# x loaded by token halves, and two of three sums of squares taken in feature order

## The chip, the cores and the metric

One core of a Trainium2 chip runs the kernel. The metric is device time in microseconds (us) of one execution; three runs of the kernel before gave 864.88, 865.59 and 865.71.

## The reference, cut to what matters

The reference is a two-layer network on x (512 tokens of 1024 features) and ctx (256 tokens). The first layer is a retention mixer, the second a gMLP mixer. The change lies in the very first step of the first layer, the norm with its modulation, and in the projections that wait for it:

```python
def rmsnorm(x, g):
    xf = x.astype(F32)
    y = xf * lax.rsqrt(jnp.mean(xf * xf, axis=-1, keepdims=True) + NORM_EPS)
    return (y * g.astype(F32)).astype(x.dtype)
...
shift_x, scale_x, gate_x = jnp.split(silu_c @ ada_w[i] + ada_b[i], 3, axis=-1)
shift_c, scale_c, gate_c = jnp.split(silu_cc @ ada_w[i] + ada_b[i], 3, axis=-1)
hx = rmsnorm(x, norm_g[i]) * (1 + scale_x[:, None]) + shift_x[:, None]
hc = rmsnorm(ctx, norm_g[i]) * (1 + scale_c) + shift_c
```

Each token thus needs the sum of the squares of its 1024 features before anything of it can be projected.

## The kernel before, in words

x and ctx come with the features on the 128 partitions: eight feature tiles `kb` of 128, `KT` = 8. x's 512 tokens are two halves of 256 (`th` 0 and 1). Four tiles `xs` hold two feature tiles each, all 512 tokens; two tiles `cq` hold four feature tiles of ctx each.

**Exact products by splitting.** Weights and activations are split into a high part (a cast on ScalarE) and a low part (a subtraction on VectorE), and a product takes three matmuls (`mm3`, L126). `Stream` (L155) loads the weights as raw pieces and splits them ahead of their use; `w11` and `w12` are the first two pieces, cut by `cut` (L795) in slices since the first products want them early. Nearly every instruction is issued through `Queue`, so the profile puts it on L54.

**The first stage** (L812 to L913) works feature tile by feature tile. One turn for `kb` is:

- `ada0_mm` (L638): the modulation's columns of that tile, c and c_ctx against the ada weights, on TensorE; then a copy `adae` on ScalarE;
- `ada0_cols` (L654): transposes of `adae` on TensorE, sums over their groups and three small operations on VectorE, giving scale `gs0` and shift `sh0`;
- `come` (L751): for one or more halves, x times scale times `rs` (VectorE, `xs<-xs,gs,rs`), plus shift (ScalarE, `oA` or `oS` for the first and the second half), and the low part (VectorE);
- `plain` (L776): the products of that tile, for half `th` and piece `nh`, added up in four PSUM banks; `features_first` (L395) takes the three matmuls in another order than `features` (L385).

`rs[t]` is one over the root mean square of each token: t = 0 and 1 are x's halves, 2 is ctx. `half_rows` (L605) gets it by transposing four feature tiles at a time on TensorE (16 transposes for a half of x, 16 for ctx) and summing squares of 128 tokens' rows: on ScalarE (Square with an accumulator) for the one 128 tokens, on VectorE (`bn_stats`) for the other. `inverse` (L616) joins the sums, takes the root (ScalarE) and the reciprocal (VectorE). `spread` (L626) brings the 256 numbers to all partitions by two products with the identity matrix, and `copied` copies them out of PSUM.

**What sets the order.** In this stage the order on TensorE, ScalarE and VectorE is that of the text (`kept`): each engine is a queue, and what waits holds up all behind it. Loads are issued by SyncE in the text's order, eight in flight at most over SyncE and ScalarE. ada tiles 4, 5 and 6 use the memory of tiles 0, 1 and 2, so their loads wait for those tiles' products. Two small loads, `cv` (c and c_ctx) and `ident` (the identity matrix), go over ScalarE's queue. ScalarE loads a table, takes Silu of `cv`, and then loads the table that Square and Sqrt use. Ten products of ones warm TensorE up at the start (`fill`), six more stand ahead of the first real products.

In the text before, both halves' statistics come first; then each turn serves both halves: tile 0 of half 0, tile 0 of half 1, then their second weight piece, then tile 1 of both, and so on.

## Time and profile before

| | |
|---|---|
| median of three runs | 865.59 us (864.88 to 865.71) |
| the profiled execution's own time | 865.68 us |
| its span, first to last instruction | 863.8 us |
| mean granted TensorE clock | 0.998 |
| TensorE, VectorE, ScalarE busy | 854.3, 706.7, 479.5 us |
| loads of x: 4, 512 KB each | 5.5 us from issue to landing (median) |
| loads of ctx: 2, 512 KB each | 8.7 us |

A span begins with the first instruction; times in the timeline count from there. PE is TensorE's matmuls, PEld its weight loads, DVE is VectorE, ACT is ScalarE, SP is SyncE, POOL is GpSimd. In a timeline a row is start, duration, engine, line, operation, what it writes and reads, its shape and how many in a row; in brackets stands how long the engine was idle before and what ended that. A product in plain float32 shows as two records, one for each pass.

### The profile page before, as it was taken

What the parts mean: (1) busy time and instruction counts of PE and PEld (TensorE: products, weight loads), DVE (VectorE), ACT (ScalarE), POOL (GpSimd) and SP (SyncE); (2) the same over time, 40 slices, a digit from 0 to 9 for tenths busy, and PEclk for the clock granted to TensorE, in tenths of its full rate; (3) what the DMA queues carried; (4) which work ended last, traced back from release to release, by engine and by line L of the source; (5) the groups of instructions that cost most, each with busy time, mean ns of one, the idle gap of its engine ahead of it and who ended that gap; (6) DMA issues with size and microseconds to landing.
All of it is one profiled execution on the core that took longest, in us unless ns stands there. A gap on an engine that the chain in (4) does not pass through costs nothing.

```text
span 863.8 us, 17055 instructions
## 1 busy us (share of the span) xinstructions
PE 854.3 (99%) x6820; PEld 816.9 (95%) x6820; DVE 706.7 (82%) x996; ACT 479.5 (56%) x763; POOL 84.8 (10%) x127
## 2 busy tenths in 40 slices
PE   8999999999999999999999999999999999999997
PEld 7899999999999999899999899999999899899985
DVE  4799899869977985799787889998888478678895
ACT  5466644455355446567872559654667456255434
POOL 0001211211211011000001011111000000000110
PEclk9999999999999999999999999999999999999999
DMA  9945857866967796248486842657556156156522
GB/s 358 405 133 147 256 174 257 259 202 197 307 205 232 223 324 235 73 122 243 157 283 174 255 113 97 232 149 230 160 148 205 39 148 219 26 152 190 122 46 101
DMA packets 78990, 164.03 MB, mean 190 GB/s; under 512 B 8256, under 2 KB 35264, under 8 KB 78912
## 3 DMA queue, kind: packets, MB, share of 16 engines
q1 hardware_dynamic: 66144, 122.37, 42.2%
q0 software_dynamic: 12336, 40.38, 18.6%
q8 instruction: 53, 0.87, 0.4%
q10 hardware_dynamic: 432, 0.20, 0.1%
q14 instruction: 25, 0.20, 0.1%
HBM read 124.65 MB, written 24.12 MB: 172 GB/s over the span
## 4 chain that ended last, share of the span: by engine, by line
PE 95%; DMA 3%; ACT 1%; DVE 1%; issue 0%; DVEq 0%; SPq 0%; ACTq 0%
PE pst L54 95%; DMA ada_w<-in_ada_dram 2%; DMA cq<-in_cT_dram 1%; DMA cv<-in_cv_dram 0%; DVE o L54 0%; ACT junk L54 0%; DVE ada_h L54 0%; ACT og L54 0%; ACT ada_h L54 0%; ACT fss L54 0%; ACT o L54 0%; DVE fss L54 0%; DVEq L1946 0%; SPq L54 0%; ACT ones_r L54 0%
## 5 line engine op out<-in xcount | busy, mean ns | idle before, releaser
L54 DVE TENSOR_TENSOR hl<-raw,hl 128x1024 fp32r<-128x1024 f32 (+2 forms) x203 | 242.8, 1200 | 74.1 <-ACT hl L54 73.5
L54 ACT CAST hl<-raw 128x1024 fp32r<-128x1024 f32 (+2 forms) x203 | 208.3, 1031 | 144.2 <-PE pst L54 63.2
L54 PE MATMUL pst<-oS,hl 128*128 128x256 f32 x1296 | 155.4, 278 | 0.0
L54 PEld LDWEIGHTS pst<-oS,hl 128*128 128x128 f32 x1296 | 151.0, 188 | 0.9 <-issue 0.8
L54 PE MATMUL pst<-hl,oS 128*128 128x256 f32 x1152 | 135.2, 277 | 0.0
L54 PE MATMUL pst<-oA,hl 128*128 128x256 f32 x1080 | 134.5, 280 | 0.1
L54 PEld LDWEIGHTS pst<-hl,oS 128*128 128x128 f32 x1152 | 133.0, 188 | 0.8 <-issue 0.4
L54 PEld LDWEIGHTS pst<-oA,hl 128*128 128x128 f32 x1080 | 128.0, 188 | 2.1 <-ACT oS L54 0.4
L54 PE MATMUL pst<-hl,oA 128*128 128x256 f32 x768 | 92.4, 277 | 0.0
L54 DVE TENSOR_TENSOR raw<-raw 128x1024 f32<-128x1024 f32 x73 | 89.0, 1220 | 0.8
L54 PEld LDWEIGHTS pst<-hl,oA 128*128 128x128 f32 x768 | 89.4, 188 | 0.0
L54 ACT ACTIVATE snap<-pst 128x512 f32<-128x512 f32 x81 | 48.2, 595 | 73.1 <-PE pst L54 73.1
L54 PE MATMUL pst<-v,ph 128*128 128x512 f32 x192 | 59.8, 393 | 0.0
L54 PE MATMUL pst<-hl,ya 128*128 128x512 f32 (+1 forms) x246 | 59.1, 386 | 0.0
L54 DVE TENSOR_TENSOR snap<-snap,pst 128x512 f32<-128x512 f32 x75 | 51.1, 681 | 4.8 <-PE pst L54 4.5
L187 POOL DMA_DIRECT2D raw<-raw x27 | 23.5, 869 | 314.3 <-DVE raw L54 228.0
L54 PEld LDWEIGHTS pst<-hl,ya 128*128 128x128 f32 x246 | 45.3, 188 | 9.5
L54 PE MATMUL pst<-og,hl 128*128 128x256 f32 x384 | 46.3, 280 | 0.0
L54 PEld LDWEIGHTS pst<-og,hl 128*128 128x128 f32 x384 | 45.0, 188 | 0.2
L54 PEld LDWEIGHTS pst<-v,ph 128*128 128x128 f32 x192 | 36.1, 188 | 7.0
L54 PE MATMUL pst<-v,pl 128*128 128x512 f32 x96 | 37.8, 394 | 0.0
L54 ACT CAST ph<-pf 128x512 fp32r<-128x512 f32 x24 | 14.9, 621 | 40.3 <-DVE pf L54 40.3
(225 smaller groups left out, 1102.4 us busy)
## 6 DMA issues: line engine op xcount, KB each, us to landing
raw<-in_w_dram SPq DMA_DIRECT2D x224, 256.0 KB, 3.8
bg<-in_adag_dram SPq DMA_DIRECT2D x32, 512.0 KB, 5.2
raw<-raw POOLq DMA_DIRECT2D x27, 512.0 KB, 5.3
ada_w<-in_ada_dram SPq DMA_DIRECT2D x16, 512.0 KB, 8.7
raw<-in_w_dram SPq DMA_DIRECT2D x16, 512.0 KB, 4.3
v<-snap POOLq DMA_DIRECT2D x16, 256.0 KB, 4.8
z<-snap POOLq DMA_DIRECT2D x16, 256.0 KB, 4.3
v<-v SPq DMA_DIRECT2D x8, 512.0 KB, 6.0
```

The source lines that it names most:

```text
L54: made = op(*args, **kw)
L187: nc.gpsimd.dma_start(self.raws[q, to], self.raws[q, src], accum_op=ALU.add)
```

## The change

1. **Loads.** `xs` comes in two rounds of four loads of 256 KB, half 0 first, each in two runs of 1 KB a partition. Order on SyncE: half 0, `sv`, ada tile 0, both first weight pieces, ada tile 1, half 1, ada tiles 2 and 3. On ScalarE's queue `ident` stands ahead of `cv`.
2. **Half 1 of x and ctx.** The transposes go. ScalarE squares the tiles as they lie (four squares of 128x512), VectorE adds them up (three additions of 128x512, one of 128x256), and two products with a single column of ones sum over the partitions and bring 128 tokens each to the partitions (`roots`). Half 0 keeps its transposes.
3. **Order.** Half 0's tiles 0 and 1 go first, each with both weight pieces. Half 1's squares stand on ScalarE in the turn of tile 1; its `roots`, the ada product of tile 2 and its `spread` follow on TensorE, and then tile 0 of half 1. From tile 2 on both halves go together as before. ctx's squares and additions stand where its transposes' statistics stood; its `roots` stand just ahead of its `spread`.

TensorE from the second ada product on, up to the ada products of tiles 3 and 4. `oA11` is half 0 and `oS3` half 1; the two `hl` are the weight pieces w11 and w12; `adae` rows are transposes of `ada0_cols`. Before:

```order
L54 MATMUL pst_340<-ada_w_152,cpad_175 32x256 x8
L54 MATMUL pst_357<-oS3_349,hl_317 128x256 x6
L54 MATMUL pst_367<-ident_130,adae_353 128x128 x2
L54 MATMUL pst_375<-oA11_328,hl_364 128x256 x6
L54 MATMUL pst_382<-oS3_349,hl_364 128x256 x6
L54 MATMUL pst_397<-ada_w_158,cpad_175 32x256 x8
L54 MATMUL pst_333<-oA11_328,hl_317 128x256 x6
L54 MATMUL pst_357<-oS3_349,hl_317 128x256 x6
L54 MATMUL pst_446<-ident_130,adae_406 128x128 x2
```

And now, from the second ada product as well:

```order
L54 MATMUL pst_320<-ada_w_155,cpad_179 32x256 x8
L54 MATMUL pst_332<-ident_130,adae_329 128x128 x2
L54 MATMUL pst_303<-oA11_298,hl_290 128x256 x6
L54 MATMUL pst_313<-oA11_298,hl_310 128x256 x6
L54 MATMUL pst_370<-ones_126,sqx_340 128x1 x2
L54 MATMUL pst_375<-ada_w_162,cpad_179 32x256 x8
L54 MATMUL pst_386<-ident_130,sq_191 128x128 x2
L54 MATMUL pst_400<-oS3_392,hl_290 128x256 x6
L54 MATMUL pst_407<-oS3_392,hl_310 128x256 x6
L54 MATMUL pst_436<-ident_130,adae_384 128x128 x2
```

Between the second ada product and the transposes of the third turn stood five groups of products of alternating halves; now there stand two groups of half 0, the one-column products, the third ada product and the spread, and then two groups of half 1.

VectorE in the same place. Before, from the second turn's scaling (`gs0`) on:

```order
L54 SCALAR_TENSOR_TENSOR gs0_182<-gs0_182,sv_128 128x2
L54 SCALAR_TENSOR_TENSOR xs_133<-xs_133,gs0_182,rs0_302 128x256
L54 SCALAR_TENSOR_TENSOR xs_133<-xs_133,gs0_182,rs1_355 128x256
L54 TENSOR_TENSOR hl_317<-raw_149,hl_317 128x2x128
L54 SCALAR_TENSOR_TENSOR oA11_328<-xs_133,sh0_183,oA11_328 128x256
L54 SCALAR_TENSOR_TENSOR oS3_349<-xs_133,sh0_183,oS3_349 128x256
L54 TENSOR_TENSOR hl_364<-raw_155,hl_364 128x2x128
L54 TENSOR_TENSOR hl_317<-raw_149,hl_317 128x2x256
L54 TENSOR_REDUCE ada_s_449<-pst_446 128x4
```

And now, from the scaling of half 0's tile 1 on (`sqx` are the squares):

```order
L54 SCALAR_TENSOR_TENSOR xs_133<-xs_133,gs0_186,rs0_269 128x256
L54 TENSOR_TENSOR hl_290<-raw_149,hl_290 128x2x128
L54 SCALAR_TENSOR_TENSOR oA11_298<-xs_133,sh0_187,oA11_298 128x256
L54 TENSOR_TENSOR hl_310<-raw_152,hl_310 128x2x128
L54 TENSOR_TENSOR sqx_340<-sqx_340,sqx_342 128x512
L54 TENSOR_TENSOR sqx_348<-sqx_348,sqx_350 128x512
L54 TENSOR_TENSOR sqx_340<-sqx_340,sqx_348 128x512
L54 TENSOR_TENSOR sqx_340<-sqx_340 128x256
L54 RECIPROCAL sq_191<-sq_191 128x2
L54 SCALAR_TENSOR_TENSOR xs_133<-xs_133,gs0_186,rs1_389 128x256 x2
L54 TENSOR_TENSOR hl_290<-raw_149,hl_290 128x2x256
L54 SCALAR_TENSOR_TENSOR oS3_392<-xs_133,sh0_187,oS3_392 128x256 x2
```

The four additions and the reciprocal stand behind the low part of w12 and ahead of half 1's first two scalings, which stood in the same turns as half 0's before.

TensorE at ctx. Before, from the ada products of tiles 5 and 6 on, the transposes of ctx (`cq`) and, later, its spread (`sq_188`):

```order
L54 MATMUL pst_596<-ada_w_421,cpad_175 32x256 x8
L54 MATMUL pst_615<-ident_130,cq_137 128x128 x4
L54 MATMUL pst_622<-ident_130,cq_137 128x128 x4
L54 MATMUL pst_628<-ident_130,cq_138 128x128 x4
L54 MATMUL pst_635<-ident_130,cq_138 128x128 x4
L54 MATMUL pst_333<-oA12_570,hl_549 128x256 x6
L54 MATMUL pst_652<-ident_130,adae_613 128x128 x4
...
L54 MATMUL pst_686<-ada_w_430,cpad_175 32x256 x4
L54 MATMUL pst_697<-ident_130,sq_188 128x128 x2
L54 MATMUL pst_333<-oA12_570,hl_549 128x256 x6
```

And now:

```order
L54 MATMUL pst_586<-ada_w_423,cpad_179 32x256 x8
L54 MATMUL pst_303<-oA12_560,hl_539 128x256 x6
L54 MATMUL pst_623<-ident_130,adae_603 128x128 x4
...
L54 MATMUL pst_657<-ada_w_432,cpad_179 32x256 x4
L54 MATMUL pst_668<-ones_126,sqx_605 128x1 x2
L54 MATMUL pst_673<-ident_130,sq_192 128x128 x2
L54 MATMUL pst_303<-oA12_560,hl_539 128x256 x6
```

The 16 transposes are gone from behind the ada products, and two one-column products stand directly ahead of the spread, which waits for their root and reciprocal.

The diff, cut to its core:

```diff
+    nc.scalar.dma_start(ident, id_d)
     nc.scalar.dma_start(cv, cv_d)
-    nc.scalar.dma_start(ident, id_d)
-    for i in range(4):
-        load(xs[i], xT_d[:, 2 * i:2 * i + 2, :])
+    def x_load(th):
+        for i in range(4):
+            load(xs[i][:, :, th * HS:th * HS + HS], xT_d[:, 2 * i:2 * i + 2, th * HS:th * HS + HS])
+    x_load(0)
     load(sv, sv_d)
     ada0_load(0)
     Q.stage = 1
     Q.pump_n(1)
+    Q.pump_n(1)
     ada0_load(1)
-    Q.pump_n(1)
+    x_load(1)
...
+    squares = []
+    def squared(x):
+        t = t2("sqx")
+        act.activation(t.rearrange("p (a n) -> p a n", a=2), x, AF.Square)
+        squares.append(t)
+    def added():
+        a, b, c, d = squares
+        squares.clear()
+        dve.tensor_tensor(a, a, b, ALU.add)
+        dve.tensor_tensor(c, c, d, ALU.add)
+        dve.tensor_tensor(a, a, c, ALU.add)
+        dve.tensor_tensor(a[:, 0:HS], a[:, 0:HS], a[:, HS:], ALU.add)
+        return a
+    def roots(t, a):
+        pr = pt((P, 2), tag="tm")
+        for i in range(2):
+            mm(pr[:, i:i + 1], a[:, i * P:i * P + P], ones[:, 0:1], start=True, stop=True, skip_group_check=True)
+        s = sq[t]
+        act.activation(s[:, 1, :], pr, AF.Sqrt, bias=eps, scale=1.0 / D)
         dve.reciprocal(s[:, 1, :], s[:, 1, :])
...
-    x_rows(0, 0)
-    x_rows(1, 0)
-    x_rows(0, 1)
-    inverse(0)
-    x_rows(1, 1)
+    for g in range(2):
+        half_rows(lambda k: xk(0, g, k), g)
+    inverse()
+    rs[0] = copied(spread(0), "rs0")
     es = ada0_mm(0)
-    rs[0] = copied(spread(0), "rs0")
-    inverse(1, lambda: ada0_cols(0, es))
+    ada0_cols(0, es)
     w11 = Q.begin()
     low = cut(w11, 0, 1)
     fill(6)
-    rs[1] = pr = spread(1)
     come((0, 0), then=low)
     plain(0, 0, (0,), features_first)
-    es = ada0_mm(1, then=lambda: come((0, 1)))
-    rs[1] = copied(pr, "rs1")
-    plain(0, 1, (0,), features_first)
     w12 = Q.begin()
     cut(w12, 0, 1)()
+    plain(0, 0, (1,), features_first)
+    es = ada0_mm(1)
+    low = cut(w11, 1, 2)
     ada0_cols(1, es)
-    plain(0, 0, (1,), features_first)
-    plain(0, 1, (1,), features_first)
-    come((1, 0), (1, 1), then=cut(w11, 1, 2))
+    half1 = xp(1, 0) + xp(1, 1)
+    for x in half1[:2]:
+        squared(x)
+    come((1, 0), then=low)
+    for x in half1[2:]:
+        squared(x)
+    cut(w12, 1, 2)()
+    plain(1, 0, (0,), features_first)
+    total = added()
+    plain(1, 0, (1,))
+    roots(1, total)
     es = ada0_mm(2)
-    cut(w12, 1, 2)()
-    cut(w11, 2, 4)()
+    rs[1] = copied(spread(1), "rs1")
+    come((0, 1), (1, 1), then=cut(w11, 2, 4))
+    plain(0, 1)
...
-    plain(1, 0, (0,), features_first)
-    plain(1, 1, (0,))
     ada0_cols(2, es)
     come((2, 0), (2, 1))
     cut(w12, 2, 4)()
-    plain(1, 0, (1,))
-    plain(1, 1, (1,))
+    plain(1, 1)
...
         if kb == 3:
             es = ada0_mm(5, 6)
-            half_rows(lambda k: cq[0][:, k, :], 0, 2)
-            half_rows(lambda k: cq[1][:, k, :], 1, 2, "tm")
-            inverse(2)
+            for c in cq:
+                squared(c[:, 0:2, :])
+                squared(c[:, 2:4, :])
+            total = added()
         if kb == 4:
             es = ada0_mm(7)
+            roots(2, total)
```

More of the change, by code (lines that the diff above doesn't have):

```diff
@@ L599, in hybrid_kernel, with half_rows @@
     sh0 = st([P, KT, 2], "sh0")
-    bnx = st([P, 3, 2, 6], "bns", name="bnx")
-    mvx = st([P, 3, 2], "mv", name="mvx")
+    bnx = st([P, 2, 6], "bns", name="bnx")
+    mvx = st([P, 2], "mv", name="mvx")
     sq = [st([P, 2, 2], f"sq{t}", name="sq") for t in range(3)]
-    def half_rows(at, g, t, tag="ps"):
+    def half_rows(at, g):
         for i in range(2):
-            pq = pt(tag=tag)
+            pq = pt()
             for k in range(4):
@@ L611, in half_rows, with inverse @@
             if i == 0:
-                act.activation(t2("junk0"), pq, AF.Square, scale=1.0 / 32.0, accum_out=sq[t][:, g, 0:1])
+                act.activation(t2("junk0"), pq, AF.Square, scale=1.0 / 32.0, accum_out=sq[0][:, g, 0:1])
             else:
-                dve.bn_stats(bnx[:, t, g, :], pq)
-    def inverse(t, then=None):
-        s, mv = sq[t], mvx[:, t, :]
-        dve.bn_aggr(mv, bnx[:, t, :, :])
+                dve.bn_stats(bnx[:, g, :], pq)
+    def inverse():
+        s, mv = sq[0], mvx
+        dve.bn_aggr(mv, bnx)
         dve.scalar_tensor_tensor(s[:, 1, 1:2], mv[:, 0:1], mv[:, 0:1], mv[:, 1:2], ALU.mult, ALU.add)
@@ L621, in inverse @@
         act.activation(s[:, 1, :], s[:, 1, :], AF.Sqrt, bias=eps, scale=1.0)
-        if then:
-            then()
+        dve.reciprocal(s[:, 1, :], s[:, 1, :])
+    squares = []
[17 more added lines that the diff above has]
+        act.activation(s[:, 1, :], pr, AF.Sqrt, bias=eps, scale=1.0 / D)
         dve.reciprocal(s[:, 1, :], s[:, 1, :])
@@ L807, in cut @@
         return low
-    def x_rows(t, g):
-        half_rows(lambda k: xk(t, g, k), g, t)
-    x_rows(0, 0)
-    x_rows(1, 0)
-    x_rows(0, 1)
-    inverse(0)
-    x_rows(1, 1)
+    for g in range(2):
+        half_rows(lambda k: xk(0, g, k), g)
+    inverse()
+    rs[0] = copied(spread(0), "rs0")
     es = ada0_mm(0)
-    rs[0] = copied(spread(0), "rs0")
-    inverse(1, lambda: ada0_cols(0, es))
+    ada0_cols(0, es)
     w11 = Q.begin()
```

## Prediction

> **What bounds it now.** I read the page first, then the chain of waits in order of time, TensorE's waits in the first 60 us, and the timeline of the first 60 us. From the page, the span and the engines' totals:
>
> ```profile
> span 863.8 us, 17055 instructions
> PE 854.3 (99%) x6820; PEld 816.9 (95%) x6820; DVE 706.7 (82%) x996; ACT 479.5 (56%) x763; POOL 84.8 (10%) x127
> ```
>
> TensorE is idle for 863.8 − 854.3 = 9.5 us in all, so what an edit takes off another engine is worth nothing unless TensorE stood for it. From the chain (start, duration, what):
>
> ```profile
> 5.07 6.47 DMA ada_w<-in_ada_dram
> ...
> 27.54 8.16 DMA cq<-in_cT_dram
> ...
> 35.84 154.11 PE pst L54 x1362
> ```
>
> Up to 35.8 us the chain is mostly loads; behind it TensorE runs for 154 us without a break. So a microsecond lost or won ahead of the unbroken stretch is passed on to the end. But the chain goes back through queued transfers. TensorE's own waits, 0 to 60 us, say how long it really stood for loads:
>
> ```profile
> PE pst L54 <- DMA ident<-in_id_dram: 0.9, 1, 0.9
> PE pst L54 <- DMA cq<-in_cT_dram: 0.5, 1, 0.5
> ```
>
> So loads are not the limit: from 15 to 41 us TensorE always has something, because products of the two halves of x alternate, and one half's products cover the other engines' work for the next tile. The change touches just that.
>
> **Rows for the sum.** The timeline (start, duration; x2 and the like: so many in a row). First the start:
>
> ```profile
> 5.14 0.22 ACT L54 ACTIVATE cpad<-cv 128x16 f32<-128x16 f32 x1 [1.98 <-DMA cv<-in_cv_dram]
> ...
> 6.62 2.16 PE L54 MATMUL pst<-ident,xs 128*128 128x128 f32 x18 [0.93 <-DMA ident<-in_id_dram]
> ...
> 7.29 0.60 ACT L54 ACTIVATE junk<-pst 128x512 f32<-128x512 f32 x1 [0.42 <-PE pst L54]
> ...
> 8.16 0.60 ACT L54 ACTIVATE junk<-pst 128x512 f32<-128x512 f32 x1 [0.18 <-PE pst L54]
> ...
> 8.66 0.19 ACT L54 ACTIVATION_READ_ACCUMULATOR junk<-pst 128x1 f32 x1
> ...
> 11.00 0.15 DVE L54 TENSOR_TENSOR sq<-sq 128x1 f32<-128x1 f32 x1
> ...
> 11.52 0.17 DVE L54 RECIPROCAL sq<-sq 128x2 f32<-128x2 f32 x1 [0.36 <-ACT sq L54]
> ...
> 11.59 0.64 PE L54 MATMUL pst<-ada_w,cpad 128*32 128x256 f32 x8 [0.30 <-DMA ada_w<-in_ada_dram]
> ...
> 14.88 1.03 PE L54 MATMUL pst<-oA,hl 128*128 128x256 f32 x6
> ```
>
> Then the pieces of one turn (ada product, copy, transposes, column sums, scaling, shift, products), and the nearest rows to what is added:
>
> ```profile
> 15.84 1.07 PE L54 MATMUL pst<-ada_w,cpad 128*32 128x256 f32 x16
> ...
> 16.97 0.37 ACT L54 COPY adae<-pst 128x256 f32<-128x256 f32 x1 [0.69 <-PE pst L54]
> ...
> 17.64 0.38 PE L54 MATMUL pst<-ident,adae 128*128 128x128 f32 x2
> ...
> 19.69 0.42 DVE L54 TENSOR_TENSOR hl<-raw,hl 128x256 fp32r<-128x256 f32 x1
> ...
> 22.30 0.38 PE L54 MATMUL pst<-ident,adae 128*128 128x128 f32 x2
> ...
> 24.68 0.60 ACT L54 CAST hl<-raw 128x512 fp32r<-128x512 f32 x1
> ...
> 25.32 0.69 DVE L54 TENSOR_TENSOR hl<-raw,hl 128x512 fp32r<-128x512 f32 x1
> ...
> 32.38 1.93 PE L54 MATMUL pst<-ada_w,cpad 128*32 128x256 f32 x32
> ...
> 34.24 1.09 PE L54 MATMUL pst<-ident,cq 128*128 128x128 f32 x8
> ...
> 35.46 0.58 ACT L54 COPY adae<-pst 128x512 f32<-128x512 f32 x1
> 35.59 1.23 DVE L54 TENSOR_TENSOR hl<-raw,hl 128x1024 fp32r<-128x1024 f32 x1 [2.15 <-ACT hl L54]
> ```
>
> ```profile
> 39.03 0.17 DVE L54 TENSOR_REDUCE ada_s<-pst 128x8 f32<-128x32 f32 x1
> ...
> 39.63 0.88 DVE L54 SCALAR_TENSOR_TENSOR xs<-xs,gs,rs 128x256 f32<-128x256 f32 x2
> ...
> 40.16 0.91 ACT L54 ACTIVATE oA<-xs,sh 128x256 fp32r<-128x256 f32 x2 [1.24 <-DVE xs L54]
> 40.70 0.88 DVE L54 SCALAR_TENSOR_TENSOR oA<-xs,sh,oA 128x256 fp32r<-128x256 f32 x2 [0.18 <-ACT oA L54]
> ...
> 41.03 0.71 PE L54 MATMUL pst<-ident,sq 128*128 128x128 f32 x4
> ...
> 41.50 2.98 PE L54 MATMUL pst<-oA,hl 128*128 128x256 f32 x24
> ...
> 54.37 2.02 ACT L54 COPY held<-pst 128x512 f32<-128x512 f32 x4
> ```
>
> Read off: column sums to scaling 0.60, scaling to shift 0.53, shift to its low part 0.54; squares of 128x512 at 0.60 each, a new one every 2.02/4 = 0.50; VectorE additions of 128x512 at 0.69, of 128x256 at 0.42; twelve products 2.98/2 = 1.5; what follows a spread starts 0.47 after it.
>
> **A. The start, to the end of the second ada product.** The loads, from two windows (the last column is GB/s; only loads in runs of 1 KB lie in the second):
>
> ```profile
> 5.00:11.00 6.00, 4.88 (x44) 4.02 (x42) 2.44 (x5) 3.77 (x9) 0.00 (x0) 1.00 1.03 413
> 42.50:49.00 6.50, 6.50 (x60) 6.50 (x59) 6.07 (x19) 3.13 (x7) 0.00 (x0) 1.00 1.05 338
> ```
>
> Ahead of the first ada tiles now lies 1.05 MB less of x (2.5 us at 413 GB/s), and the 1.05 MB that stays comes in runs of 1 KB, at 338 instead of 413: 0.6 more. The first ada tiles' end moves from 11.55 (chain) to 9.6. TensorE doesn't get to use that: the spread now stands ahead of the ada product in its queue, and behind ScalarE's Squares, which stand behind the table load, which stands behind cv. cv changes places with ident on ScalarE's queue and lands between 5.1 and 6.6 (where the two rows show them): the first Square at 7.3 to 8.7; I take 7.5, near the lower end, since cv is small. Two Squares with their reads end 8.85 − 7.29 = 1.56 later, at 9.1; addition to reciprocal 11.69 − 11.00 = 0.7, 9.8; spread, and 0.47 on the ada product (1.07) to 11.3. From its end to the first product 14.88 − 12.23 = 2.65: 13.95, against 14.88. Then twelve products of one half at 13.95 to 15.65, and the second ada product there instead of at 15.84. **A = −0.2** (−0.8 with cv at once; +1.1 with cv at 6.6). The 16 transposes of x's second half that go, and their statistics on ScalarE and VectorE, cost nothing today: they lie ahead of an ada product that waits 0.30 for its load.
>
> **B. From there to the third turn's transposes.** Before, 16.91 to 22.30 = 5.4 us, in which TensorE does five groups of six products, of both halves, and the third ada product. Now, counted from the end of the second ada product: copy to 0.45, transposes to 0.85, column sums at 0.9, scaling at 1.5, shift at 2.05; ScalarE then does the last two squares (2.5 to 3.6) and the cast of a weight piece (to 3.95), VectorE its low part (to 4.35). Only then come the additions, which stand behind that low part on VectorE: 0.69, 0.60 for the second on its heels, 0.69, 0.42: done at 6.8. The one-column products, priced as a spread until the next starts (0.47), to 7.3; the third ada product to 8.35, with root and reciprocal beside it; spread 0.71, copy 0.37: 9.5; scaling, and shift at 10.05; VectorE's second scaling (0.4), a weight's low part (0.69) and the shift's low part (0.48) to 11.5; the twelve products of second half, tile 0 (1.5, all but the first need it) to 12.9. Only then stand the third turn's transposes. 12.9 − 5.4: **B = +7.5**. TensorE stands three times: some 2 us in the turn's chain, uncovered now, 2 for the additions, 2.5 for the spread's copy, scaling and shift.
>
> The one-column products' wait holds up the third ada product, and with it, on SyncE's queue, the loads of the seventh ada tiles, which take over the third ones' place:
>
> ```profile
> ada_w<-in_ada_dram SPq DMA_DIRECT2D x16, 512.0 KB, 8.7
> ```
>
> Some 8.7 us after an issue near 25 they are there at 34, and are asked for near 40 (32.38 before): no cost, with 6 us of cover. x's second half comes behind the second ada tiles (1.05 MB, 3.1 us at 338 GB/s), near 18, and the last squares ask at 16.7 + 2.5 = 19.2: no cost, with 1 us of cover.
>
> Bounds of B: +6.3 if the additions overlap the casts and one-column products cost half; +8.4 if each hand-over costs 0.1 more.
>
> The Trainium skill (TensorE: Matmul & The Clock Gate, "Back-to-back issue gap") puts a product of up to 64 columns at about 60 cycles against 134 for 128 columns; no row here shows one column. By it the one-column products would end about 0.1 sooner, and the sum would be 0.1 less.
>
> From the third turn's transposes to the ada product of tiles 5 and 6 (22.30 to 32.38) nothing is reordered: no term.
>
> **C. ctx.** From 32.38 to the products of tile 5 (the sixth) at 41.50: 9.1 us. The 16 transposes go (two times 1.09), and also the wait of 0.5. In their place: copy at 2.0 after 32.38, four squares behind it on ScalarE, the last ending at 2.0 + 0.5 + 1.5 + 0.6 = 4.6; additions 0.69, 0.69, 0.42 behind it to 6.45; tile 5's column sums, which stand behind them on VectorE, at 6.5, no later than before (39.03 − 32.38 = 6.65); scaling 7.1, shift 7.6 to 8.5; ScalarE's copy of the last ada product, then the root (it stands behind both), to 9.1; reciprocal 9.3; spread; products at 9.8. **C = +0.7**: what TensorE no longer transposes it waits for the root, which before lay far ahead of the spread. Bounds −0.3 (root slips in front) to +1.2.
>
> **Sum.** −0.2 + 7.5 + 0.7 = +8.0. The profiled execution took 865.68 (863.8 and 1.9 around the span), 0.09 above the median of 865.59; against the median 865.6 + 8.0 = **873.6 us**. Later nothing gives it back: TensorE has no pause there to shrink.
>
> **Rivals.**
> 1. *Loads are the real limit and swallow the delay* (faster). The chain of waits speaks for it. The second weight piece of tile 4 is ready at 35.59 + 1.23 = 36.8 whatever TensorE does, and TensorE's transposes of ctx, 2.2 us, are gone; a delay under about 1.1 us would be lost there and about 1.0 us gained: 864.6. It decides at 1.1 us of delay; I count 7.3 (A + B) by then, and the waits above show 0.5 us for that load. Chance 6%.
> 2. *A smaller loss:* the additions run in gaps and the two halves overlap more than the order lets me believe; half of B, 865.6 − 0.2 + 3.75 + 0.7 = 869.9. Chance 9%, and 3% for within 0.2%.
> 3. *The clock falls in the pauses.* The start shows the two paces:
>
> ```profile
> 1.05 4.64 PE L54 MATMUL pst<-ones 128*128 128x128 f32 x20 [1.05 <-DVE eps L54]
> ...
> 12.99 1.50 PE L54 MATMUL pst<-ones 128*128 128x128 f32 x12
> ```
>
> 0.23 us each at first, 0.125 later. If the pauses of 2 and 2.5 us brought back the slow pace for as long as the first fill shows (4.6 us), the products behind the longest pause, 1.5 + 1.5 us, would take twice that: +3, 876.6. Against it: the granted clock stays 1.00 in the windows above. The Trainium skill (TensorE: Matmul & The Clock Gate, "What's actually happening") has the array fall to half after an idle window of about 3.4 us; by it 2.5 us is not enough. Chance 7%.
>
> **Numbers.** Forecast (A + B + C within bounds: 865.6 + 5.2 to + 10.7, so 870.8 to 876.3) 75%. The range 869.0 to 876.8 takes in those bounds, rival 2's figure and rival 3's; rival 1 and no change stay outside, and what the bounds may have missed. About 0.2% (1.7 us) is what a measurement of this kernel can tell from no change. Faster 6%, within 0.2% 3%, slower 91%.
>
> **What would show it.** In the changed profile: TensorE's waits in 10 to 50 us rise by 6 us or more, three pauses of about 2 us each ahead of 30 us and a fourth ahead of ctx's spread, released by ACT oA, DVE sqx and ACT oS; the one-column product near 23 us, the third turn's transposes near 29.6 (22.30 before); products of tile 5 near 49.5 (41.50); granted clock 1.00. Wrong if the third turn's transposes stand before 25, if squares or additions are done while products of the other half run, or if time after 60 us changes.

## The result, and the profile after

The changed kernel takes 877.00 us (median of four runs, 876.56 to 877.51) against 865.24 (864.40 to 865.71) for the kernel before, measured beside it: a ratio of 1.0137, 95% interval 1.0125 to 1.0149. That is +11.8 us, where +8.0 was forecast, just above the upper end of the range, 876.8. The profiled execution took 877.51 us.

The page of the changed kernel, span and engines' totals:

```profile
span 875.7 us, 17010 instructions
PE 857.8 (98%) x6796; PEld 818.0 (93%) x6796; DVE 708.0 (81%) x994; ACT 481.4 (55%) x763; POOL 84.9 (10%) x127
```

TensorE does 24 instructions fewer than before and is busy 3.5 us longer (857.8 against 854.3), and idle 17.9 us instead of 9.5. So there are two losses to look for: pauses, +8.4, and the same work done more slowly, +3.5. TensorE's waits in the first 70 us (total, times, longest):

```profile
PE pst L54 <- DVE sq L54: 3.7, 2, 1.9
PE pst L54 <- ACT oA L54: 1.7, 1, 1.7
PE pst L54 <- ACT oS L54: 1.5, 1, 1.5
...
PE pst L54 <- DVE sqx L54: 0.8, 1, 0.8
```

What ends the pauses is what the forecast named (ACT `oA`, DVE `sqx`, ACT `oS`), no pause is longer than 1.9, and no wait for a load is among the large ones. The timeline (start, duration; x2 and the like: so many in a row):

```profile
6.87 0.87 PE L54 MATMUL pst<-ident,xs 128*128 128x128 f32 x6 [0.30 <-DMA xs<-in_xT_dram]
...
7.78 0.70 DVE L54 BATCH_NORM_STATS2 bnx<-pst 128x6 f32<-128x512 f32 x1 [0.93 <-PE pst L54]
...
9.63 0.71 PE L54 MATMUL pst<-ident,sq 128*128 128x128 f32 x4 [1.89 <-DVE sq L54]
...
12.50 2.42 PE L54 MATMUL pst<-ones 128*128 128x128 f32 x12
...
16.23 1.07 PE L54 MATMUL pst<-ada_w,cpad 128*32 128x256 f32 x16
...
19.95 1.02 PE L54 MATMUL pst<-oA,hl 128*128 128x256 f32 x6 [1.72 <-ACT oA L54]
...
21.61 2.47 DVE L54 TENSOR_TENSOR sqx<-sqx 128x512 f32<-128x512 f32 x4
...
24.23 0.98 PE L54 MATMUL pst<-ones,sqx 128*128 128x1 f32 x4 [0.83 <-DVE sqx L54]
25.14 1.93 PE L54 MATMUL pst<-ada_w,cpad 128*32 128x256 f32 x16
...
29.75 0.58 PE L54 MATMUL pst<-oS,hl 128*128 128x256 f32 x1 [1.52 <-ACT oS L54]
30.60 2.72 PE L54 MATMUL pst<-oS,hl 128*128 128x256 f32 x11 [0.28 <-DVE oS L54]
33.12 0.63 PE L54 MATMUL pst<-ident,adae 128*128 128x128 f32 x2
...
44.05 1.93 PE L54 MATMUL pst<-ada_w,cpad 128*32 128x256 f32 x32
...
53.27 0.71 PE L54 MATMUL pst<-ident,sq 128*128 128x128 f32 x4 [1.81 <-DVE sq L54]
53.73 2.98 PE L54 MATMUL pst<-oA,hl 128*128 128x256 f32 x24
```

Two things stand in these rows. The order is that of the forecast: additions (21.61), one-column products (24.23), third ada product, half 1's tile 0 (29.75), and only then the third turn's transposes. And many rows take twice their price: twelve products of ones 2.42 instead of 1.50, an ada product 1.93 at 25.14 but 1.07 at 16.23, eleven products 2.72 where twelve cost 1.5. The granted clock says why. Windows of the same execution (busy time and number of instructions of PE, PEld, DVE, ACT, POOL; then the granted TensorE clock, the DMA share and GB/s):

```profile
7.59:11.00 3.41, 1.52 (x22) 0.94 (x20) 1.36 (x5) 1.11 (x4) 0.00 (x0) 1.00 0.96 336
11.00:14.41 3.41, 2.94 (x19) 2.39 (x12) 1.35 (x6) 1.15 (x4) 0.00 (x0) 0.50 1.04 415
...
17.83:21.24 3.41, 1.42 (x8) 0.98 (x8) 1.84 (x7) 3.10 (x7) 0.00 (x0) 1.00 1.02 413
21.24:24.65 3.41, 2.08 (x9) 1.81 (x9) 2.75 (x5) 0.00 (x0) 0.00 (x0) 0.50 1.03 420
24.65:28.07 3.42, 3.42 (x23) 1.99 (x23) 0.17 (x1) 0.63 (x2) 0.00 (x0) 0.50 1.02 408
28.07:31.48 3.41, 1.61 (x6) 1.17 (x6) 2.27 (x5) 1.80 (x4) 0.00 (x0) 0.50 1.01 350
31.48:34.89 3.41, 3.41 (x18) 3.41 (x18) 1.04 (x6) 0.00 (x0) 0.00 (x0) 0.50 0.91 284
```

From 11.00 to 14.41 and from 21.24 to 34.89, 17.1 us in all, TensorE ran at half pace. Each of the two stretches follows a window of 3.41 us in which TensorE was busy for 1.52 or 1.42 us. The pause of 1.81 ahead of ctx's spread brought no half pace in this execution: the 24 products behind it take their usual 2.98. Before the change the clock is at 1.00 from 6 us to the last products.

Against the kernel before, the sum in the forecast's own pieces (start of a row to start of a row):

| piece | before | after | difference | forecast |
|---|---|---|---|---|
| A: to the end of the second ada product | 16.91 | 17.30 | +0.4 | −0.2 |
| B: from there to the third turn's transposes | 5.39 | 15.82 | +10.4 | +7.5 |
| to the ada product of tiles 5 and 6 | 10.08 | 10.93 | +0.9 | 0 |
| C: to the products of tile 5 | 9.12 | 9.68 | +0.6 | +0.7 |
| sum | 41.50 | 53.73 | +12.2 | +8.0 |

Later stretches are shifted by 11.3 to 12.2 us and give little back.

### The profile page after: what moved, and what is told of

Same layout as the page of the kernel before. It is cut to its first block, busy times and chain, and to the rows that moved or that the text cites. A ratio compares the mean times of both kernels' runs of the same rounds, so it can differ in the third digit from the quotient of the medians.

```text
span 875.7 us, 17010 instructions
## 1 busy us (share of the span) xinstructions
PE 857.8 (98%) x6796; PEld 818.0 (93%) x6796; DVE 708.0 (81%) x994; ACT 481.4 (55%) x763; POOL 84.9 (10%) x127
## 4 chain that ended last, share of the span: by engine, by line
PE 95%; DVE 2%; ACT 1%; DMA 1%; issue 0%; SPq 0%; DVEq 0%; ACTq 0%
PE pst L54 95%; DMA xs<-in_xT_dram 1%; DVE sqx L54 0%; ACT sqx L54 0%; DVE o L54 0%; ACT junk L54 0%; DVE xs L54 0%; SPq L54 0%; DVE ada_h L54 0%; ACT og L54 0%; DVE hl L54 0%; ACT oA L54 0%; ACT ada_h L54 0%; DVE oA L54 0%; ACT fss L54 0%
## 5 line engine op out<-in xcount | busy, mean ns | idle before, releaser
L54 PE MATMUL pst<-oS,hl 128*128 128x256 f32 x1296 | 157.6, 280 | 1.8 <-ACT oS L54 1.5
L54 PEld LDWEIGHTS pst<-oS,hl 128*128 128x128 f32 x1296 | 152.9, 190 | 2.9 <-ACT oS L54 1.8
```

The costliest lines, as they stand in the source:

```text
L54: made = op(*args, **kw)
```

## The experiments

The theory to be tested: the new order costs about 8 by uncovered hand-overs, and the half clock that its pauses bring on costs 3 to 4 more. The main rival: the hand-overs cost all of it, and a TensorE that waits for others loses nothing by running slowly.

### 1. All pauses of the x part filled

```
+    fill(6)
     rs[0] = copied(spread(0), "rs0")
...
     ada0_cols(1, es)
+    fill(6)
...
     plain(1, 0, (0,), features_first)
+    fill(2)
     total = added()
     plain(1, 0, (1,))
+    fill(4)
     roots(1, total)
...
     come((0, 1), (1, 1), then=cut(w11, 2, 4))
+    fill(6)
     plain(0, 1)
```

`fill(n)` is n products of ones whose result nobody reads; nothing waits for them but what stands behind them on TensorE.

> The changed kernel, with products of ones put into TensorE's pauses (6 ahead of half 0's spread, 6 behind the second turn's transposes, 2 between the two weight pieces of tile 1, 4 ahead of the one-column products, 6 ahead of half 1's tile 0). Nothing else moves. Theory (the pauses of the new order cost about 8, and the slow clock that they bring on, at half pace from 11.0 to 14.4 and from 21.2 to 34.9, costs 3 to 4 more): the granted clock stays at 1.00 from 5 us on, the third turn's transposes come at 29.5 to 30.5 (33.1 without the fillings), and the time is 873.4 (872.8 to 874.3), against 877.0. Rival (all 11.8 are the uncovered hand-overs, and a TensorE that waits for others loses nothing by running slowly): 876.5 to 877.5, or more, since the fillings stand ahead of real work.

Measured: 874.26 us (873.39 to 874.86), ratio 1.0111 (1.0096 to 1.0127), inside the theory's range. More work on TensorE made the kernel 2.7 us faster than the changed one, so the rival falls. In the profiled execution the third turn's transposes stand at 29.82. The four executions still scatter by 1.5 us: the pause of 1.81 ahead of ctx's spread is not filled here.

### 2. The same without the first six

```
-    fill(6)
     rs[0] = copied(spread(0), "rs0")
```

> As the run with all fillings, without the six ahead of half 0's spread. Theory: the clock still falls from about 11.0 to 14.4, which costs the six fillings and first products there some 0.7, and no longer falls at 21.2: 874.1 (873.4 to 874.9). Rival (nothing of it is the clock): as the changed kernel, 876.5 to 877.5. A third case, that the first fall brings on the second, would show a second cold stretch in spite of the fillings, and 876 or more.

Measured: 875.12 us (874.65 to 876.45), 0.2 above the range given. In the profiled execution the first pause, 1.88 us long as in the changed kernel, brought no half pace at all; the pause ahead of ctx's spread did, from 50.60 to 54.01. So one and the same pause lowers the clock in one execution and not in another. The rows price the first stretch all the same: from the start of half 0's spread to the end of the second ada product it is 7.14 here (9.78 to 16.92) and 7.67 in the changed kernel (9.63 to 17.30), in the same order of the same work. The first stretch at half pace costs 0.5.

### 3. All pauses filled, ctx's too

```
             roots(2, total)
+            fill(8)
```

(on top of experiment 1)

> The changed kernel with all fillings and eight products of ones (2.0 us) more in the pause ahead of ctx's spread, so that no long pause is left unfilled. Theory (what is left of the loss with the clock at full pace throughout is the forecast's own sum, +8.0): in all executions the clock is at 0.998 or more, and the time is that of the fastest executions with fillings before, 873.2 (872.4 to 873.9); between executions it varies by less than the 1.5 us seen before. Rival (the fillings help by something other than the clock, or ctx's pause is harmless): 874.3 as before, with a scatter as before.

Measured: 872.61 us, and now 872.55 to 872.96 only, inside the theory's range; the kernel before took 864.88 beside it; ratio 1.0090 (1.0074 to 1.0107). The scatter is down to 0.4, and 4.4 us of the changed kernel's 877.0 are gone (4.0 if each is counted against the kernel before measured beside it: +11.8 and +7.7). Its timeline:

```profile
15.75 1.07 PE L54 MATMUL pst<-ada_w,cpad 128*32 128x256 f32 x16
...
29.72 0.38 PE L54 MATMUL pst<-ident,adae 128*128 128x128 f32 x2
...
39.78 1.93 PE L54 MATMUL pst<-ada_w,cpad 128*32 128x256 f32 x32
...
49.47 2.98 PE L54 MATMUL pst<-oA,hl 128*128 128x256 f32 x24
```

In the forecast's pieces: A ends at 16.82 (−0.1); B is 29.72 − 16.82 = 12.90 (+7.5); the next piece 10.06 (0.0); C 9.69 (+0.6). The sum is +8.0, piece by piece close to the forecast's. What the changed kernel has beyond that is the clock: +0.5 in A, +2.9 in B, +0.9 behind it.

### 4. Pauses of many lengths in the unbroken stretch

```
+    def pause(k):
+        g, p = t2("gap"), pt()
+        nc.gpsimd.memset(g, 1.0)
+        mm(p[:, 0:P], ones, g[:, 0:P], start=True, stop=True, skip_group_check=True)
+        for j in range(k):
+            nc.gpsimd.memset(g, 1.0)
+        mm(p[:, P:2 * P], ones, g[:, 0:P], start=True, stop=True, skip_group_check=True)
```

(in the kernel before, at 18 places of the projections, k from 1 to 6)

> The kernel before with 18 pauses put into TensorE's unbroken stretch (60 to 300 us), 12 us or more apart: a product of ones that waits for one to six fillings of a 128x512 tile by GpSimd, which wait for TensorE in their turn. It asks how long a pause has to be for the clock to fall. Theory (what counts is the busy share of a window of 3.41 us, and below 0.45 to 0.48 of it the next window is at half pace): pauses under 1.8 us never bring a half-pace window, those of 1.9 to 2.7 do in some cases (where one window holds nearly all of the pause), those of 3 us and more nearly always; each half-pace window lasts 3.41 us and costs dense products 1.6 to 1.7 us beside the pause. Rival (a pause must be as long as a whole window, 3.4 us): no half-pace window behind any pause under 3.4 us.

Measured: 952.53 us (950.50 and 954.56). The 18 pauses are 0.64 to 6.32 us long, 51.3 in all. No half pace followed the five of 0.64 and 1.23, nor those of 2.28, 2.48 and 2.88; it followed those of 1.81 and 2.97 and all eight of 3.43 and more, for one or two windows of 3.41. The two that decide, first a pause that did nothing and then one that did (rows of the timeline, then windows that start where the clock's own steps lie):

```profile
145.26 0.49 PE L54 MATMUL pst<-gap,ones 128*128 128x128 f32 x2 [2.88 <-POOL gap L1200]
...
344.67 0.65 PE L54 MATMUL pst<-gap,ones 128*128 128x128 f32 x2 [1.81 <-POOL gap L1200]
```

```profile
140.07:143.48 3.41, 2.31 (x21) 2.12 (x19) 3.38 (x6) 1.83 (x3) 0.98 (x2) 1.00 0.47 147
143.48:146.89 3.41, 1.63 (x14) 1.64 (x15) 3.41 (x5) 0.08 (x1) 1.62 (x4) 1.00 0.60 201
146.89:150.31 3.42, 3.42 (x33) 3.42 (x32) 1.22 (x3) 1.51 (x4) 0.37 (x1) 1.00 0.77 274
341.46:344.87 3.41, 1.60 (x14) 1.41 (x13) 2.63 (x3) 1.53 (x2) 1.83 (x4) 1.00 0.70 199
344.87:348.28 3.41, 3.41 (x17) 3.41 (x17) 0.65 (x1) 0.00 (x0) 0.21 (x1) 0.50 0.90 284
```

A pause of 2.88 that two windows share leaves 1.63 us busy in the emptier one, and nothing happens; one of 1.81 that lies in one window leaves 1.60, and the next 3.41 us hold 17 products instead of 33. So in this run it is the busy share of a fixed window that counts, near 0.47, and where the window's edges fall decides; the last section has windows of other runs that busy time alone does not explain. The rival that a pause must fill a whole window falls.

### 5. The changed kernel without half 1's sum

```
     plain(1, 0, (0,), features_first)
-    total = added()
     plain(1, 0, (1,))
-    roots(1, total)
     es = ada0_mm(2)
-    rs[1] = copied(spread(1), "rs1")
+    rs[1] = rs[0]
```

(and no `squared` for half 1)

> The changed kernel without half 1's sum of squares: no squares, additions, one-column products, root and spread of half 1; half 1 is scaled with half 0's roots instead (so half 1's norm is left out). The order of the products stays. Theory: of the three pauses the two of the sum go (2.0 and 2.5 by the forecast, with 0.7 of spread), the one in the second turn's own chain stays: 877.0 - 5 = 872.0; with no cold stretch at 21.2 to 34.9 left, some 2 to 3 less: 869.5; range 869 to 872.5. Rival (the loss is in the order of the halves itself, tile 1 of half 0 alone with nothing beside it, and in the loads by halves, and the sum is hidden): 875 to 877.

Measured: 872.12 us (870.88 to 873.86), 4.9 below the changed kernel and 7 above the one before, inside the theory's range. From the end of the second ada product to the third turn's transposes the profiled execution takes 10.66 (16.45 to 27.11), against 15.82 with the sum and 5.39 before the change. The sum's chain, half pace included, is thus about half of B's loss. The other half stays: with the sum gone, tile 0 and 1 of half 0 still go alone, with nothing of half 1 beside them, and in the profiled execution one window at half pace (24.55 to 27.97) is left. The rival's 875 or more is out.

### 6. The loads as before

```
-    x_load(0)
+    for i in range(4):
+        load(xs[i], xT_d[:, 2 * i:2 * i + 2, :])
...
-    x_load(1)
```

(in the kernel of experiment 1; cv, ident and the first weight pieces in their old order too)

> The changed kernel with all fillings (874.3), but with the loads as before: x whole in four loads of 512 KB ahead of everything, cv ahead of ident, first weight piece, second ada tile, second weight piece. Theory (the loads by halves are a gain by themselves, which the new order of the sums eats up): half 0's spread stands near 12 instead of 9.8, the first product near 16.5 instead of 14.2, and the time is 874.3 + 2.3 = 876.6 (875.6 to 877.6). Rival (the loads by halves cost or bring nothing, or cost because runs of 1 KB move slower): 873 to 874.8.

Measured: 878.04 us (877.17 to 878.49), 3.8 above experiment 1 and 0.4 above the range given. Half 0's spread stands at 11.63 instead of 9.79, the third turn's transposes at 32.58 instead of 29.82, so 2.8 are the loads; the profile also has a window at half pace from 52.59 to 56.00, behind ctx's unfilled pause, which experiment 1's profile has not. The loads by halves are a gain of 2.8 in this order, and the order eats it up.

### 7. ctx's part undone, the rest filled

```
-            for c in cq:
-                squared(c[:, 0:2, :])
-                squared(c[:, 2:4, :])
-            total = added()
+            half_rows(lambda k: cq[0][:, k, :], 0, 2)
+            half_rows(lambda k: cq[1][:, k, :], 1, 2, "tm")
+            inverse(2)
```

(in the kernel of experiment 1, with `roots(2, total)` gone)

> The changed kernel with the first set of fillings, but ctx's part undone: ctx's 16 transposes, their statistics and spread as before the change. What is left is the change to the loads and to x. Theory (sums A and B, -0.2 and +7.5, and no pause ahead of ctx's spread, so no half clock there): 864.7 + 7.4 = 872.1 (871.3 to 873.2), some 1 to 2 below the kernel with the same fillings and ctx's part in (874.3). Rival (ctx's part is harmless inside the change, since the loads of ctx and of the second weight piece have more time there): 873.8 to 874.8.

Measured: 870.99 us (870.74 to 871.23), +6.1 on the kernel before, 1.6 below experiment 3 and 0.3 below the range given. From its timeline:

```profile
39.47 1.93 PE L54 MATMUL pst<-ada_w,cpad 128*32 128x256 f32 x32
...
47.91 2.98 PE L54 MATMUL pst<-oA,hl 128*128 128x256 f32 x24
```

With the transposes the piece takes 8.44 (39.47 to 47.91), not 9.12 as before the change: the delay ahead of it swallows the wait for ctx's load, 0.5 before. With the squares it takes 9.69. So ctx's part costs 1.25 where it stands; 0.6 is only what shows against before.

### 8. ctx's part alone

```
-            half_rows(lambda k: cq[0][:, k, :], 0, 2)
-            half_rows(lambda k: cq[1][:, k, :], 1, 2, "tm")
-            inverse(2)
+            for c in cq:
+                squared(c[:, 0:2, :])
+                squared(c[:, 2:4, :])
+            total = added()
         if kb == 4:
             es = ada0_mm(7)
+            roots(2, total)
```

(in the kernel before)

> The kernel before, with only ctx's part of the change (squares, additions and one-column products in place of the 16 transposes and their statistics; spread where it was). Theory: what TensorE no longer transposes it waits for, behind the squares on ScalarE and the additions on VectorE: +0.6 (+0.1 to +1.0), so 865.9 beside 865.3. Rival (ctx's part is a gain by itself, and the 0.56 more that the trace shows there belong to the cold clock or the delayed loads): -1.0 to -2.2, so 863.1 to 864.3.

Measured: 869.21 us (867.73 to 870.44), +4.2 on 865.01: neither theory nor rival. Timeline and windows:

```profile
42.44 0.71 PE L54 MATMUL pst<-ident,sq 128*128 128x128 f32 x4 [1.81 <-DVE sq L54]
42.91 4.58 PE L54 MATMUL pst<-oA,hl 128*128 128x256 f32 x24
```

```profile
39.74:43.16 3.42, 1.58 (x18) 1.24 (x11) 2.40 (x10) 1.33 (x4) 0.00 (x0) 1.00 1.09 378
43.16:46.57 3.41, 3.41 (x18) 3.41 (x18) 2.98 (x8) 1.76 (x5) 0.00 (x0) 0.50 1.10 348
```

The wait for the root puts tile 5's products 1.4 later than before (41.50), and the half pace behind it makes 24 products cost 4.58 instead of 2.98. By the next stage that is 3.0 (58.45 against 55.44); a further 1.5 is lost near 648 us (experiment 11). The executions go with the clock: 867.73 at a mean of 0.999, 870.44 at 0.996.

### 9. The same, with that pause filled

```
             roots(2, total)
+            fill(8)
```

> The kernel with ctx's part alone, and eight products of ones (2.0 us) in the pause ahead of ctx's spread. Theory: the wait itself stays (tile 5's products at 42.9 to 43.2, against 41.5 before), the clock stays at 1.00 behind it, and the 24 products there take 2.98 again, not 4.58: 869.2 - 2.0 = 867.2 (866.4 to 868.0), beside 865.0. Rival (the slower products are not the clock's doing but those of loads or of the other engines): 868.8 to 870.

Measured: 867.08 us (ten runs, 865.78 to 868.20), ratio 1.0026 (1.0017 to 1.0035), inside the theory's range. The products behind the pause:

```profile
42.96 2.99 PE L54 MATMUL pst<-oA,hl 128*128 128x256 f32 x24
```

They start where they did without the filling and take their usual time. The loss falls from +4.2 to +2.2, and the 1.6 that these products no longer cost are the clock. The ten executions spread over 2.4 us at mean clocks of 0.998 and 0.999, so this scatter is not the clock's.

### 10. ctx's sum a turn later

```
-    CTX_COME = {4: (0, 1, 2), 5: (3, 4), 6: (5, 6, 7)}
-    CTX_PLAIN = {5: (0, 1, 2), 6: (3, 4), 7: (5, 6, 7)}
+    CTX_COME = {5: (0, 1, 2), 6: (3, 4, 5, 6, 7)}
+    CTX_PLAIN = {6: (0, 1, 2), 7: (3, 4, 5, 6, 7)}
...
+        if kb == 4:
+            for c in cq:
+                squared(c[:, 0:2, :])
+                squared(c[:, 2:4, :])
+            total = added()
...
+        if kb == 5:
+            roots(2, total)
...
-        if kb == 4:
+        if kb == 5:
             rs[2] = copied(spread(2), "rs2")
```

> The kernel before, with ctx summed by squares, additions and one-column products as in the change, but a turn later: squares and additions behind tile 5's shift, one-column products and spread behind tile 5's products and the next, ctx's own products from tile 6's turn on; the second weight piece of tiles 4 to 7 is loaded ahead of ctx. Theory (the squares are no loss by themselves; the +4.2 of ctx's part alone is a pause of 1.8 ahead of the spread, the waits around it, and the half clock behind it): no pause is left, TensorE no longer does 16 transposes (2.2) or waits 0.5 for ctx, so -1.0 to -2.5: 863.3 (862.5 to 864.2) beside 865.0, and the clock at 1.00 from 6 us on. Rival (squares, additions and column products cost more on ScalarE and VectorE than the transposes cost TensorE, wherever they stand): 865.5 to 869.

Measured: 868.26 us (867.67 to 868.73), +3.4 on 864.83: not the theory's 863.3 but inside the rival's 865.5 to 869. The spread again:

```profile
44.24 0.71 PE L54 MATMUL pst<-ident,sq 128*128 128x128 f32 x4 [1.26 <-DVE sq L54]
```

The root stands on ScalarE behind tile 6's two shifts, its reciprocal on VectorE behind their low parts; a wait of 1.26, and half pace from 45.39 to 48.81, behind a window that was busy for 1.99 of 3.41 us. At 57.54 the next stage begins 2.1 later than before the change (55.44); a further 1.4 is lost near 648 us (experiment 11).

### 11. ctx's sum later still

```
+    CTX_COME = {6: ((0, 1, 2), (3, 4, 5, 6, 7))}
+    CTX_PLAIN = {7: range(8)}
...
         plain(kb, 0, (1,))
+        if kb == 6:
+            rs[2] = copied(spread(2), "rs2")
...
+        if kb == 5:
+            roots(2, total)
```

(squares and additions as in experiment 10; the one-column products now stand behind both halves' products of tile 5)

> As the run with ctx's sum a turn later, which came out at 868.3 because the spread still waited 1.3 for the root behind tile 6's shift and the half clock followed: now the one-column products stand behind all products of tile 5, the spread in tile 6's turn behind half 0's products, and all of ctx is scaled in tile 6's turn and multiplied in tile 7's. Theory: no pause of over 0.5 is left between 25 and 60, the clock stays at 1.00, and what is saved is the 16 transposes with their wait, 2.2 to 2.7, less the one-column products (0.6): 863.1 (862.5 to 864.0), beside 864.8. Rival (the path through ctx's sum is always longer than the transposes): 865.5 to 868.

Measured: 866.95 us (866.41 to 867.23), ratio 1.0026 (1.0016 to 1.0036), inside the rival's 865.5 to 868. Between 25 and 60 us no pause of over 0.5 and no half pace is left, and still there is no gain. Its timeline, and one row of its waits from 60 us on:

```profile
32.89 1.93 PE L54 MATMUL pst<-ada_w,cpad 128*32 128x256 f32 x32
...
39.18 3.09 PE L54 MATMUL pst<-oA,hl 128*128 128x256 f32 x24
...
43.28 1.38 PE L54 MATMUL pst<-oA,hl 128*128 128x256 f32 x6 [0.27 <-ACT oA L54]
...
55.97 0.88 PE L54 MATMUL pst<-hl,oA 128*128 128x256 f32 x6
...
647.97 1.59 ACT L54 ACTIVATE vt<-vt,nm,rv 128x256 f32<-128x256 f32 x3 [2.31 <-DMA vt<-vt]
```

```profile
PE pst L54 <- ACT snap L54: 1.1, 1, 1.1
```

The same first product of the next stage, and the same row of ScalarE, in the kernel before:

```profile
55.44 0.87 PE L54 MATMUL pst<-hl,oA 128*128 128x256 f32 x6
...
646.46 1.59 ACT L54 ACTIVATE vt<-vt,nm,rv 128x256 f32<-128x256 f32 x3 [0.80 <-DMA vt<-vt]
```

Tile 5's products come 2.3 us earlier than before (39.18 against 41.50), 0.5 of it because the spread no longer stands ahead of them, and by 56 us all of it is gone. From the ada product of tiles 5 and 6 to the next stage the run takes 23.08 (32.89 to 55.97), the kernel before 23.06 (32.38 to 55.44): the gain of the missing transposes goes into the one-column products and the pauses beside them (1.0, from 42.27 to 43.28), into tile 6's first six products, 1.38 instead of 0.84 (46.36 in the kernel before), since their tile waits behind the additions on VectorE, and into smaller delays behind. Moved this far, ctx's sum neither wins nor loses. The 0.5 at 55.97 is there at 32.89 already, behind a wait of 0.41 for an ada tile.

The 1.1 of the waits' row lies far from ctx's part. At 641.04 both profiled executions start the same product; some 13 us later this one is 1.4 behind (656.17 against 654.74). ScalarE waits 2.31 instead of 0.80 for a transfer of `vt`, and TensorE then waits for ScalarE's copy `snap`. The profiles of experiments 8, 10 and 12 have the same (2.22 to 2.36, and 1.05 to 1.19 on TensorE), that of experiment 9 a shorter wait (1.50 and 0.33); in the changed kernel and in experiments 3 and 7 ScalarE waits 0.76 to 0.90 and TensorE not at all. In the DMA records of experiments 8, 10, 11 and 12, and of none of the others, a packet of 16 KB of the instruction queue starts 3.4 to 3.5 us after the transfer's issue, while its own packets run. That this packet holds the transfer up fits, but was not tested. The rest up to +2.4 is the profiled execution of before, 865.68, against the median of the runs beside this one, 864.57.

### 12. Half 1's sum in the old order

```
     x_rows(0, 0)
-    x_rows(1, 0)
     x_rows(0, 1)
     inverse(0)
-    x_rows(1, 1)
+    for x in xp(1, 0) + xp(1, 1):
+        squared(x)
     es = ada0_mm(0)
     rs[0] = copied(spread(0), "rs0")
-    inverse(1, lambda: ada0_cols(0, es))
+    total = added()
+    ada0_cols(0, es)
...
-    rs[1] = pr = spread(1)
     come((0, 0), then=low)
+    roots(1, total)
     plain(0, 0, (0,), features_first)
+    rs[1] = pr = spread(1)
```

> The kernel before, in its own order of loads and products, with only half 1's statistics replaced by squares, additions and one-column products; its one-column products stand ahead of the first real products, its spread behind them. Theory: in this order the sum is covered by half 0's work, so the hand-overs cost nothing: third turn's transposes at 21.5 to 23 (22.3 before), and 864.8 (864.2 to 866.0); if the 16 transposes that go leave a window of TensorE under half busy near 9 to 12 us, the half clock adds 0.5 to 1.5. Rival (squares, additions and one-column products are slower than transposes wherever they stand): 867 or more.

Measured: 868.71 us (867.91 to 869.32), +4.1 on 864.57: not the theory's 864.8 but the rival's figure, 867 or more. The start of its timeline:

```profile
12.01 2.17 ACT L54 ACTIVATE sqx<-xs 128x512 f32<-128x512 f32 x4
...
14.09 0.35 ACT L54 COPY adae<-pst 128x256 f32<-128x256 f32 x1
14.21 1.88 DVE L54 TENSOR_TENSOR sqx<-sqx 128x512 f32<-128x512 f32 x3 [0.35 <-ACT sqx L54]
...
16.01 0.17 DVE L54 TENSOR_REDUCE ada_s<-pst 128x4 f32<-128x16 f32 x1
...
17.75 1.02 PE L54 MATMUL pst<-oA,hl 128*128 128x256 f32 x6 [0.93 <-ACT oA L54]
```

The first product comes at 17.75 instead of 14.88, the third turn's transposes at 25.63 instead of 22.30: the four squares stand ahead of the copy of the ada product on ScalarE, the additions ahead of its column sums on VectorE. The sum was not covered in this place either; a half-pace window (9.05 to 12.46) came on top, and 1.3 near 648 us (experiment 11). That it could be covered somewhere in the old order is neither shown nor excluded.

## Why the prediction was wrong

**Right, and shown.** Loads are not the limit: no large wait names one, and the time is lost where the order put it. With every pause filled the four pieces measure −0.1, +7.5, 0.0 and +0.6 against −0.2, +7.5, 0 and +0.7. For B the hand-overs come where the sum put them, counted from the end of the second ada product: one-column products at 6.9 (forecast 6.8), spread at 8.4 (8.35), the last of tile 0's products from 11.5 on (11.5), the third turn's transposes at 12.9 (12.9). The chain of squares, additions behind the weight's low part, one-column products, third ada product, spread, scaling and shift is as long as the sum made it, and taking the sum out took 4.9 away.

**A: the right figure by luck.** The forecast let half 0's spread wait for ScalarE's Squares, the first at 7.3 to 8.7, and gave A −0.8 if cv came at once. The 7.3 was read off a Square that stood 0.42 for TensorE's transposes, not for ScalarE's tables. In the changed kernel cv is there at once (Silu at 5.10) and the first Square starts at 6.74, but the spread still comes only at 9.63: the last transposes wait 0.30 for x's load (6.87), VectorE's statistics follow them (7.78), and the addition of the sums stands behind those (8.90). The Squares and their reads are done at 8.03. Two errors, a wait misread and one left out, made the −0.2.

**Wrong: the third rival was set aside.** The step that failed is that the sum has no term for the clock. It rests on the sentence "Against it: the granted clock stays 1.00 in the windows above", with the idle window of about 3.4 us behind it, and with that goes the line in "What would show it", granted clock 1.00. The windows of the kernel before have no pauses of 2 us and could say nothing of a kernel that has them; and a pause need not be as long as a window. In place of nothing the runs give 4.4 us (877.00 − 872.61; 4.0 against the kernel before measured beside each, 4.3 by the rows up to tile 5), over 17.1 us at half pace in the profiled execution. The rival had the right mechanism. That its 876.6 was only 0.4 short of the result is luck: its +3 doubles 3 us of products behind one pause, for the 4.6 us of the first fill, whereas five windows ran at half pace, and TensorE waited for others through part of them.

**Wrong in a smaller way: "from the third turn's transposes nothing is reordered: no term".** Nothing was, but the half pace lasted to 34.89 and cost 0.9 there. A term that is nothing in the order may still be something in the clock.

**C: right in size, incomplete in its account.** Against before +0.6; but the delay ahead of it also hid the wait for ctx's load (experiment 7), so that the squares cost 1.25 where they stand. Alone in the kernel before ctx's part measures +2.2 with its pause filled and +4.2 without, of which about 1.5 each are lost near 648 us (experiment 11).

**Open.** What is counted besides TensorE's busy time when the clock falls; whether half 1's sum could be covered somewhere in the old order; what delays the transfer near 648 us. None of the versions tried beats the kernel before: with the x part's pauses filled and ctx's part undone it is still 6.1 behind.

## What to carry to other kernels

A change that opens pauses of 1.5 to 2 us can cost more than the pauses, here 8 us of hand-overs and 4 of clock: look at TensorE's busy share in windows of 3.41 us, and where it would fall below half, price the next such windows at half pace, or fill the pause with products that nobody reads. A sum by squares and additions moves work from TensorE to queues on which the next tile's copy, scaling and shift stand too; what counts is what it is put in front of. When executions of one kernel scatter by more than usual, compare their mean clocks first; and before a late delay is put down to the change, see whether it begins where the change is (the 1.4 us near 648 us did not).

## What the runs showed of the hardware

- The clock changes in steps of 3.41 us, and a fall follows a window in which TensorE was busy for less than about half of it: 1.42, 1.52, 1.58 and 1.60 us brought one; 1.63, 1.67 and 1.68 did not, and 1.59 did so once (experiment 12, 5.63 to 9.05) and not another time (experiment 5, 7.49 to 10.90), so the limit lies near 0.47 and is not sharp in busy time. The Trainium skill (TensorE: Matmul & The Clock Gate, "What's actually happening") has free-running windows of 3413 ns, which the steps bear out, and a fall after at least one idle window; the pause of 1.81 us in a busy stretch shows that the window need not be idle, and the measurement decides.
- Since the windows run by themselves, one pause of 1.9 us lowers the clock in one execution and not in another (the one ahead of half 0's spread, in the changed kernel and in experiment 2), and a pause of 2.88 that two windows share does nothing.
- Half pace is not left at the share at which it begins. Windows at half pace that were busy for 1.61 and 2.08 us (changed kernel) and for 0.95, 1.62 and 2.22 us (experiment 4) were followed by another one, those busy for 2.94 us (changed kernel) and 2.99 us (experiment 4) by full pace. So the pauses ahead of 21.24 could bring four windows in a row.
- Busy time is not all that is counted. The window from 24.65 to 28.07 was busy throughout, with one-column products, an ada product of 32 columns and a spread, and the next stayed at half pace; the window of experiment 10 with one-column products and a spread was busy for 1.99 us (0.58), and the clock fell. What is counted in its place is open.
- Half pace costs dense products 1.6 us a window (24 products 4.58 instead of 2.98), but a stretch in which TensorE waits much less: 4.0 to 4.4 us for five windows.
